# Where a prefix scan gets its first factor: from its own tile's front column, written one step ahead

## The chip, the cores and the metric

The kernel runs on one core of a Trainium2 chip. The metric is the device time of one execution in microseconds (us), the median of several runs. A profile is one further execution, recorded by the hardware profiler. Its engines are PE (TensorE matmuls), PEld (TensorE weight loads), DVE (VectorE), ACT (ScalarE), POOL (GpSimd) and SP (SyncE, which issues most DMAs).

## The reference, cut to what matters

One layer of an encoder over 2048 tokens of width 1024, in float32: a normed and modulated input, one input projection, two groups of eight attention heads of width 64, an output projection with a residual, and a squared-ReLU MLP. The change lies in the first group of heads, stick-breaking attention:

```
z = einsum(q, k) * scale                        # one row per query, one column per key
log_1m_beta = where(key < query, log_sigmoid(-z), 0)
suffix = cumsum(log_1m_beta, reverse) - log_1m_beta
w = where(key < query, exp(log_sigmoid(z) + suffix), 0)
out = w @ v
```

In products instead of logarithms: with f = sigmoid(-z), a running product p over the keys, from the nearest key to the farthest, gives the weight of a key as the product in front of it minus the product behind it. The kernel computes it so. The tokens stand in reverse order, so that "towards the past" is a scan from left to right.

## The kernel before, in words

The order of the work is written out by hand. First comes the input projection of the last block of tokens with the modulation (up to about 414 us from the start of the span), then the attention (to about 1300 us), in which matmuls of the remaining projections fill TensorE between the attention's own, then the MLP.

The attention is a list `units` (lines 1151 to 1154). A unit `SB(h, g, c)` is one stick-breaking head h, a block g of 512 queries and a block c of 512 keys; for one head and query block the units c = g, g+1, ... 3 follow one another. The unit with c = g is the diagonal one (`self.diag`), the others are called carried here, since their scan goes on from the last column of the unit before. A unit `CA(h, g)` is a head of the second group with softmax. Each unit has four steps, one for each 128 queries (`qi`). There are 80 stick-breaking units with 320 steps: 128 diagonal and 192 carried.

The loop over the steps (lines 1233 to 1267) emits for step i, in this order: the transposes of the weights of a unit eight steps back (`transposes`, TensorE, into PSUM tile `wt`); `soft1` of step i; for softmax units a scale on POOL; `parts`, which splits `wt` into `wth` (ACT) and `wtl` (DVE); the jobs left by the step before (`done`: copies of a finished accumulator on ACT and its sum `o` and split `os` on POOL, sums of squares `r` on POOL, evictions of the filling matmuls on ACT and DVE); the value matmuls `acc`; `scores` of step i+1 (TensorE, into PSUM tile `z`); and some filling matmuls. `z` and `wt` share four PSUM banks (line 95, and lines 759 and 817). Each engine works through its instructions in the order in which they are emitted.

`soft1` of a stick-breaking step (lines 822 to 840) is what the change touches. It takes a tile `pt` (named `p`, 513 columns, six buffers, line 680) and a tile `w` (named `b`). ACT replaces `z` by its sigmoid. POOL copies one column into `pt[:, 0:1]`: ones on the diagonal, or else `self.carry[qi]`, the last column of the product tile of four steps before. DVE scans: its first factor is the scalar operand, 1.0 on the diagonal, or else the carried column itself, read from the older tile; its products go to `pt[:, 1:n+1]`. POOL subtracts neighbouring columns of `pt` into `w`. On the diagonal step qi covers 512 - 128 qi columns, elsewhere 512.

The lines that the profile gives for these instructions are all that of a helper that records them (L42), so they are told apart by their tiles: `p<-z,p,zero` is a carried scan, `p<-z,masked` a diagonal one, `p<-p` and `p<-ones` are the copies, `b<-p` is the subtract.

Of the kernel before, what the change touches and what calls it, by code (L numbers as in the profile page):

```python
# [9 lines left out]
F32 = mybir.dt.float32  # L10
# [8 lines left out]
P = 128  # L19
# [6 lines left out]
TB = 512  # L26
# [53 lines left out]
def encoder_kernel(ctx, tc, xT, c, g1, g2, w_in, w_rest, gqk, bias, w_o, w1, w2, w_ada, b_ada, out):  # L80
    nc = tc.nc
    act, dve, pool, sp = nc.scalar, nc.vector, nc.gpsimd, nc.sync
# [34 lines left out]
    ones = cpool.tile([P, P], F32, name="ones")  # L117
# [121 lines left out]
    if True:  # L239
# [202 lines left out]
        def load_raws(*q):  # L442

            while loads and len(raws) - sum(len(wts.get(k, ())) >= (4 if k[1] < 4 else 4 * m + 4) for k, m in raws) < 3:
                load_raw(*loads.pop(0), *q)
# [42 lines left out]
        act, dve, pool = (Ordered(tc, e) for e in (act, dve, pool))  # L488
# [124 lines left out]
        def hook(job, n):  # L613

            if (job, n) == ((0, 3, 3), 1):
                dve.tensor_scalar_mul(gqk_s[:, 0:1], gqk_sb[:, 0:1], 0.125)
                dve.tensor_copy(gqk_s[:, 1:2], gqk_sb[:, 1:2])
                for p in range(2):
                    sp.dma_start(scr_w[p,], wide[:, :, :, p, :].bitcast(F32))
            if (job, n) == ((0, 6, 3), 2):  # L620
                norms.flush()
                end_norm(2, h_tile(2), 0, KT // 2)
            if (job, n) == ((0, 6, 3), 3):
                end_norm(2, hts[2], KT // 2, KT)
            if (job, n) == ((0, 6, 2), 1):
                load_x(1)
            if (job, n) == ((0, 4, 3), 0):
                start_norm(1, 5, 3)
            if (job, n) == ((0, 10, 2), 0):
                norms.flush()  # L630
                end_norm(1, h_tile(1))
                load_x(0)
                behind.add(2, lambda: start_norm(0, 3, 2))
            if (job, n) == ((1, 6, 1), 2):
                norms.flush()
                end_norm(0, h_tile(0), 0, KT // 2)
            if (job, n) == ((1, 6, 1), 3):
                end_norm(0, hts[0], KT // 2, KT)
            if (job, n) == ((1, 6, 0), 1):
                sp.dma_start(scr_h, whole[0].bitcast(F32))  # L640

        def run_job(n):
            nonlocal credit
            key, t = jobs[n][:2], jobs[n][2]
            last = n + 1 == len(jobs) or jobs[n + 1][:2] != key
            load_raws()
            if last and key != keys[-1]:
                after = keys[keys.index(key) + 1]
                coming.extend((after, m) for m in range(len(wts.get(after, ())), count[after]))
            bank = project(key, t, hts[t], last)  # L650
            for b in range(2 if key[1] < 4 else 4):
                hook(jobs[n], b)
                next(bank)
                behind.tick()
                norms.tick()
                later.tick()
                credit += (2.4 if key[0] else 1.65) if key[1] > 3 else 1.0 * key[0]
                while todo and credit > 0:
                    cost, job = todo.pop(0)
                    job()  # L660
                    credit -= cost
            for _ in bank:
                pass
            assert not coming
# [13 lines left out]
    if True:  # L678
        kp0 = ph.enter_context(tc.tile_pool(name="kp0", bufs=3, side="right"))
        zp = ph.enter_context(tc.tile_pool(name="zp", bufs=6, side="right"))  # L680
# [66 lines left out]
        class Unit:  # L747


            def __init__(self, h, g, first, last):  # L750
                self.h, self.g, self.first, self.last = h, g, first, last
                self.nm = f"{self.ca}_{h}_{g}"
                self.ws = []
                self.wt = {}

            def transposes(self, j):
                kb, q0, q1 = self.blocks[j]
                nm = f"{self.nm}_{kb}"
                wt = pz.tile([P, TB], F32, tag="z", name=f"wt{nm}")
                for qi in range(q0, q1):  # L760
                    pe.transpose(wt[:, qi * P : (qi + 1) * P], self.weights(qi, kb), ident)
                self.wt[j] = wt
# [22 lines left out]
        class SB(Unit):  # L785
# [10 lines left out]
            def load(self):  # L796
                if self.first:
                    pend["q"] = load_q(0, self.h, self.g)
                    pend["last"] = [None] * 4
                self.q = pend["q"]  # L800
                self.carry = pend["last"]
                self.k = self.shared("k", lambda: load_k(0, self.h, self.c, 1, f"{self.g}_{self.c}"))
# [4 lines left out]
            def shared(self, what, get):  # L807
# [2 lines left out]
                    pend[what] = get()  # L810
                return pend[what]

            def scores(self, qi):
                nm = f"{self.nm}_{qi}"
                c0 = qi * P if self.diag else 0
                n = TB - c0
                self.z = z = pz.tile([P, TB], F32, tag="z", name=f"z{nm}")
                qs = slice(qi * P, (qi + 1) * P)
                pe.matmul(z[:, :n], self.q[:, 0, qs], self.k[:, c0:], start=True, stop=False)
                pe.matmul(z[:, :n], self.q[:, 1, qs], self.k[:, c0:], start=False, stop=True)  # L820

            def soft1(self, qi):
                nm = f"{self.nm}_{qi}"
                c0 = qi * P if self.diag else 0
                n = TB - c0
                z = self.z
                w = zw.tile([P, TB], F32, tag="w", name=f"b{nm}")
                pt = zp.tile([P, TB + 1], F32, tag="p", name=f"p{nm}")
                act.activation(z[:, :n], z[:, :n], AF.Sigmoid, scale=-0.125)
                before = ones[:, 0:1] if self.diag else self.carry[qi]  # L830
                pool.tensor_copy(pt[:, 0:1], before)

                op, begin = (ALU.max, masked[:, :n]) if self.diag else (ALU.add, zero.to_broadcast([P, n]))
                dve.tensor_tensor_scan(
                    pt[:, 1 : n + 1], z[:, :n], begin, 1.0 if self.diag else before, op0=ALU.mult, op1=op,
                )

                pool.tensor_tensor(w[:, :n], pt[:, :n], pt[:, 1 : n + 1], op=ALU.subtract)
                self.carry[qi] = pt[:, n : n + 1]
                self.ws.append((w, c0))  # L840
# [310 lines left out]
        units = []  # L1151
# [50 lines left out]
        def value(u, j):  # L1202
            u.values(j)
# [5 lines left out]
        for _ in range(2):  # L1209
            filler[0].load()  # L1210
        run_job(len(jobs) - 1)
        units[0].scores(0)
        later.flush()
        pa.close()
# [15 lines left out]
        steps = [(u, st) for u in units for st in range(STEPS)]  # L1230

        turns = {STEPS * n: 4 if u.ca else 8 for n, u in enumerate(units) if n and u.ca != units[n - 1].ca}
        for i in range(len(steps) + LAG):
            if i % STEPS == 0:
                if i // STEPS + AHEAD < len(units):
                    load(units[i // STEPS + AHEAD])
            vi = i - VST
            if vi >= 0 and vi % STEPS == 0 and vi // STEPS < len(units):
                units[vi // STEPS].load_values()
            front, fs = steps[i] if i < len(steps) else (None, 0)  # L1240
            back, bs = steps[i - LAG] if i >= LAG else (None, 0)
            done = list(soon)
            soon.clear()
            js = []
            if back is not None:
                nb = len(back.blocks)
                js = range(nb * bs // STEPS, nb * (bs + 1) // STEPS)
            for j in js:
                back.transposes(j)
            if front is not None:  # L1250
                front.soft1(fs)
            while first:
                first.pop(0)()
            for j in js:
                back.parts(j)
                late.append((back, j))
            if front is not None:
                front.soft2(fs)
            for job in done:
                job()  # L1260
            while len(late) > AVLAG:
                value(*late.pop(0))
            if i + 1 < len(steps):
                u, st = steps[i + 1]
                u.scores(st)
            fill(front.weight if front else 0.6, turns.get(i, 0))
            later.tick()
# [26 lines left out]
    if True:  # L1294
# [35 lines left out]
        steps, jobs = [], {}  # L1330
# [514 lines left out]
        for mb in (1, 0):  # L1845
            begin = len(steps)
            steps += [First(mb, j, i) for j in range(NP) for i in OUTER]
            end = len(steps)
            for j in range(NP):
                f = steps[begin + 7 * j]  # L1850
# [33 lines left out]
        f = plain(0, 1)  # L1884
# [4 lines left out]
        for i, p in ((7, 6), (2, 5), (3, None), (4, None)):  # L1889
            f = outer(i, plan)  # L1890
# [109 lines left out]
```

## Time and profile before

| | |
|---|---|
| runs | 2566.47, 2568.27, 2568.61 us; median 2568.27 |
| the profiled execution | 2568.92 us |
| its span, first to last instruction | 2567.2 us |
| mean granted TensorE clock | 0.997 |
| scans on DVE | 192 carried, 245.7 us; 128 diagonal, 104.3 us |
| subtracts `b<-p` on POOL | 320, 292.5 us |
| copies into column 0 on POOL | 192 of a carried column, 36.0 us; 128 of ones, 23.7 us |

How to read the lines: in a list of groups, the mean duration in ns and the idle time of the engine ahead of the group follow the busy time, with what ended the idle time behind an arrow. In the order of time, a row has its start, its duration, the engine and the instruction with output and inputs; in brackets stands the idle time before it, and what ended it. Where an instruction waits for several others, the bracket names the one that came last by the profile, which can be a neighbour in time of the real one. `x2` at the end of a row means that two like instructions are merged into it.

### The profile page before, as it was taken

How to read it: one execution, taken by the hardware profiler on the slowest of the kernel's cores; microseconds unless marked ns; L12 is line 12 of the kernel's file. 1: busy time of each engine (PE TensorE's matmuls, PEld its weight loads, DVE VectorE, ACT ScalarE, POOL GpSimd, SP SyncE). 2: the span in 40 equal slices, each digit the busy share in tenths (PEclk: the TensorE clock that was granted, in tenths of full speed). 3: DMA queues.
4: the chain of work that ended last, by engine and by line, in shares of the span. 5: the costliest groups of instructions: out<-in, count | busy, mean ns of one | idle time of the engine just before them, and what ended most of it. 6: DMA issues, size and time to landing. Idle time of an engine off the chain costs nothing.

```text
span 2567.2 us, 39419 instructions
## 1 busy us (share of the span) xinstructions
PE 2534.1 (99%) x12436; PEld 2109.1 (82%) x12436; DVE 2012.0 (78%) x3501; ACT 1496.2 (58%) x2871; POOL 760.8 (30%) x1136
## 2 busy tenths in 40 slices
PE   9999999999999999999999999999999999999999
PEld 7888888888888888887887888888888878788887
DVE  7656767887789878998867777668978657988897
ACT  6333435668866687666755555566555545646565
POOL 4330145776776667777612000000000000000000
PEclk9999999999999999999999999999999999999999
DMA  9879978689877788756786888787899779677872
GB/s 351 332 298 363 342 281 293 213 237 290 277 239 233 238 279 272 248 193 196 224 309 243 286 285 274 260 306 267 275 323 304 273 254 409 246 272 265 291 268 82
DMA packets 293200, 698.92 MB, mean 272 GB/s; under 512 B 31360, under 2 KB 83584, under 8 KB 281856
## 3 DMA queue, kind: packets, MB, share of 16 engines
q1 hardware_dynamic: 291696, 691.69, 78.1%
q10 hardware_dynamic: 1296, 4.72, 0.5%
q8 instruction: 98, 1.61, 0.2%
q14 instruction: 110, 0.90, 0.1%
HBM read 477.66 MB, written 218.63 MB: 271 GB/s over the span
## 4 chain that ended last, share of the span: by engine, by line
PE 86%; DVE 5%; ACT 3%; DMA 2%; issue 2%; POOL 1%; SPq 1%; DVEq 0%; POOLq 0%; ACTq 0%
PE ps L42 29%; PE ps_s L42 14%; PE pt L42 11%; PE acc L42 6%; PE wt L42 6%; PE po L42 4%; PE z L42 4%; PE pf L42 4%; PE pq L42 3%; PE cz L42 2%; DVE p L42 2%; PE pso L42 1%; DVE opr L42 1%; PE ct L42 1%; ACT z L42 1%
## 5 line engine op out<-in xcount | busy, mean ns | idle before, releaser
L42 PE MATMUL ps<-h,opw 128*128 128x512 f32 x1512 | 361.7, 392 | 3.6 <-ACT cp L42 3.6
L42 ACT CAST wth<-wt 128x512 fp32r<-128x512 f32 (+3 forms) x544 | 257.4, 484 | 172.4 <-PE wt L42 162.5
L42 POOL TENSOR_TENSOR b<-p 128x512 f32<-128x512 f32 (+1 forms) x320 | 292.5, 914 | 167.9 <-DVE p L42 91.9
L42 PEld LDWEIGHTS ps<-h,opw 128*128 128x128 f32 x1512 | 285.7, 189 | 63.6 <-ACT cp L42 4.0
L42 DVE TENSOR_TENSOR wtl<-wt,wth 128x512 fp32r<-128x512 f32 (+3 forms) x544 | 291.2, 547 | 59.2 <-ACT wth L42 56.7
L42 PE MATMUL pt<-w,ht 128*128 128x512 f32 x1248 | 288.2, 391 | 0.0
L42 PE MATMUL ps_s<-h,opw 128*128 128x512 f32 x1152 | 278.6, 391 | 3.2 <-ACT ps_s L42 3.2
L42 PEld LDWEIGHTS pt<-w,ht 128*128 128x128 f32 x1248 | 233.0, 188 | 47.7
L42 PE MATMUL ps<-oph,opv 128*128 128x512 f32 x1152 | 263.8, 391 | 2.5 <-DVE txo L42 2.5
L42 DVE TENSOR_TENSOR_SCAN p<-z,p,zero 128x512 f32<-128x512 f32 x192 | 245.7, 1281 | 25.6 <-ACT z L42 18.6
L42 PEld LDWEIGHTS ps_s<-h,opw 128*128 128x128 f32 x1152 | 217.1, 189 | 48.8 <-ACT ps_s L42 3.6
L42 PEld LDWEIGHTS ps<-oph,opv 128*128 128x128 f32 x1152 | 217.2, 189 | 48.4 <-DVE txo L42 3.0
L42 PE MATMUL acc<-wth,v 128*128 128x512 f32 (+3 forms) x544 | 220.5, 409 | 0.0
L42 ACT CAST opr<-r 128x512 fp32r<-128x512 f32 x224 | 139.3, 623 | 107.7 <-PE ps L42 51.1
L42 ACT ACTIVATE z<-z 128x512 f32<-128x512 f32 (+1 forms) x320 | 166.5, 521 | 55.2 <-PE z L42 49.3
L42 PE MATMUL z<-k,q 128*128 128x512 f32 (+3 forms) x640 | 185.6, 372 | 7.7 <-DVE p L42 7.2
L42 PE MATMUL acc<-wtl,v 128*128 128x512 f32 (+3 forms) x544 | 185.4, 347 | 0.0
L42 PE MATMUL ps<-opr,ol 128*128 128x512 f32 x768 | 176.4, 389 | 0.1
L42 DVE TENSOR_TENSOR opr<-r,opr 128x512 fp32r<-128x512 f32 x224 | 151.2, 688 | 27.5 <-ACT opr L42 24.8
L42 PE MATMUL wt<-ident,b 128*128 128x128 f32 x1088 | 171.4, 273 | 1.1 <-DVE cols L42 0.3
L42 PEld LDWEIGHTS wt<-ident,b 128*128 128x128 f32 x1088 | 136.3, 140 | 42.2 <-DVE cols L42 1.8
L42 PEld LDWEIGHTS ps<-opr,ol 128*128 128x128 f32 x768 | 144.0, 188 | 30.5 <-DVE ol L42 0.4
(218 smaller groups left out, 4862.8 us busy)
## 6 DMA issues: line engine op xcount, KB each, us to landing
q<-scr_q SPq DMA_DIRECT2D x128, 256.0 KB, 4.7
w<-in_w_dram SPq DMA_DIRECT2D x64, 512.0 KB, 5.8
r<-scr_hid SPq DMA_DIRECT2D x64, 512.0 KB, 7.5
k<-scr_k SPq DMA_DIRECT2D x240, 128.0 KB, 4.3
v<-scr_v SPq DMA_DIRECT2D x120, 256.0 KB, 3.9
wa<-in_w_ada_dram SPq DMA_DIRECT2D x48, 512.0 KB, 6.4
ow<-scr_wo SPq DMA_DIRECT2D x24, 1024.0 KB, 5.8
hw<-scr_hid SPq DMA_DIRECT2D x48, 512.0 KB, 6.4
```

The costliest lines, as they stand in the source:

```text
L42: return lambda *x, **y: self.tc.keep_in_program_order(f(*x, **y))
```

## The change

A method `begin(qi)` takes the tile `pt` and emits the copy into its column 0. It is called for step i+1 in step i, behind the transposes and ahead of `soft1` of step i; for the very first step it is called ahead of the first scores. For softmax units it does nothing. `soft1` then picks the tile up, and a carried scan reads its first factor from `pt[:, 0:1]` and no longer from the older tile. The scalar of a diagonal scan stays the constant 1.0, as that line is not changed. The rest of `soft1` is not changed either.

```diff
+                self.pt = {}
+
+            def begin(self, qi):
+                pass
...
+            def begin(self, qi):
+                self.pt[qi] = pt = zp.tile([P, TB + 1], F32, tag="p", name=f"p{self.nm}_{qi}")
+                pool.tensor_copy(pt[:, 0:1], ones[:, 0:1] if self.diag else self.carry[qi])
+
...
-                pt = zp.tile([P, TB + 1], F32, tag="p", name=f"p{nm}")
+                pt = self.pt.pop(qi)
                 act.activation(z[:, :n], z[:, :n], AF.Sigmoid, scale=-0.125)
-                before = ones[:, 0:1] if self.diag else self.carry[qi]
-                pool.tensor_copy(pt[:, 0:1], before)
+                before = pt[:, 0:1]
...
+        units[0].begin(0)
         units[0].scores(0)
...
             for j in js:
                 back.transposes(j)
+            if i + 1 < len(steps):
+                steps[i + 1][0].begin(steps[i + 1][1])
             if front is not None:
                 front.soft1(fs)
```

## The prediction, made before the changed kernel had run

> **What bounds the kernel now.** I read the head of the profile first, then the busy time by stage, then who waits for whom, and last the order of time at the scans. All times are us from the start of the span.
>
> ```profile
> PE 2534.1 (99%) x12436; PEld 2109.1 (82%) x12436; DVE 2012.0 (78%) x3501; ACT 1496.2 (58%) x2871; POOL 760.8 (30%) x1136
> ```
>
> TensorE is busy for 99% of the span, so a change in another engine counts only where TensorE's queue, which runs strictly in program order, stands still for it. The next row is the first stage with scans, by window (its length, then busy time of PE, PEld, DVE, ACT, POOL, then the granted clock).
>
> ```profile
> 414.00:500.00 86.00, 83.73 (x469) 70.07 (x468) 74.57 (x107) 56.99 (x122) 61.15 (x117) 1.00 0.83 251
> ```
>
> DVE is busy for 74.57 of 86 us, 87%: it is the engine with the least room behind TensorE. The longest of the waits of TensorE's weight loads while scans and softmax run, and the work on the scan's tile `p`, show how the two are tied:
>
> ```profile
> PEld z L42 <- DVE p L42: 14.1, 27, 1.3
> ```
>
> ```profile
> L42 POOL TENSOR_TENSOR b<-p x320: 400/1042/1046, 416.2 to 1207.2; 128x512 f32<-128x512 f32 x128, 128x256 f32<-128x256 f32 x32
> L42 DVE TENSOR_TENSOR_SCAN p<-z,p,zero x192: 1260/1284/1289, 417.9 to 1205.8; 128x512 f32<-128x512 f32 x192
> ...
>   POOL p L42: 5.5, 9
> ```
>
> 27 times the weights of a score matmul `z` wait for a scan, 14.1 us in all, 1.3 at the longest. Four PSUM banks are shared by `z` and `wt`, one of each per step, so the scores for step k+2 take the bank that scan k frees. A late scan stops TensorE once it is later than the room before that load. The last row is idle time of DVE ahead of a scan that a copy on POOL is said to have ended: 5.5 us in 9 places, so today the scans hardly wait for POOL.
>
> **The change part by part.** *Number of instructions.* Nothing is added: one copy per scan stays, at 0.18 to 0.19 us (the COPY rows below); 320 scans and 320 subtracts stay. No DMA is issued by what is moved, and POOL issues none in this stage; SP's queue is untouched. If POOL's work were on the path, moving them would change nothing in its sum.
>
> *The copy's new place.* POOL's queue is now copy k, subtract k, whatever `done` brings (sums `o`, `os`, `r`), copy k+1, subtract k+1. After the change copy k+1 stands ahead of subtract k, behind the jobs of step k-1; that is the slot where copy k stands now. It is moved past one subtract and, where there are any, one step's `done` jobs or softmax scale. Could it hold up the subtract behind it? It needs scan k-3 and the old readers of its buffer, all older than scan k, for which that subtract waits anyway. I take 0; without this cover it would cost 0.19 us on POOL, once per step, beside a subtract.
>
> *The new wait.* A carried scan (192 of 320) reads its first factor from column 0 of its own tile, which POOL writes. Before, it took the factor from the older tile, written by DVE. Now scan k needs copy k. The diagonal scans (128) keep the constant 1.0 in the call and gain no wait. That a carried scan does not need its copy now is seen where it starts first:
>
> ```profile
> 417.91 4.81 DVE L42 TENSOR_TENSOR_SCAN p<-z,p,zero 128x512 f32<-128x512 f32 x4
> ...
> 419.09 0.19 POOL L42 COPY p<-ones 128x1 f32<-128x1 f32 x1
> ...
> 419.70 0.19 POOL L42 COPY p<-p 128x1 f32<-128x1 f32 x1
> ...
> 422.63 1.20 DVE L42 TENSOR_TENSOR_SCAN p<-z,masked 128x512 f32<-128x512 f32 x1
> ...
> 423.89 0.30 PEld L42 LDWEIGHTS z<-k,q 128*128 128x128 f32 x2 [0.30 <-DVE p L42]
> ```
>
> The scan at 417.91 runs 1.8 us ahead of its copy at 419.70. DVE may run ahead of POOL by what the six `p` buffers allow; the change cuts this to about one step. Queued behind a waiting scan on DVE are the step's `wtl` subtraction, the evictions of the dense banks (`stf`, `svf`, `xr`) and the next scan; TensorE waits for all of them.
>
> *What an ordinary step pays: nothing.*
>
> ```profile
> 714.46 0.19 POOL L42 COPY p<-p 128x1 f32<-128x1 f32 x1
> ...
> 715.48 1.28 DVE L42 TENSOR_TENSOR_SCAN p<-z,p,zero 128x512 f32<-128x512 f32 x1
> ```
>
> The scan at 715.48 would need the copy that stands where the one of 714.46 does; it ends at 714.65, 0.83 early. The cover is that step's DVE and ACT work. I made this comparison for all 192 carried scans (start against the end of the copy one place ahead, plus 0.05 for the handoff): 28 come too early, by 15.7 us in sum. The first is the one at 417.91, the last this:
>
> ```profile
> 1191.98 1.28 DVE L42 TENSOR_TENSOR_SCAN p<-z,p,zero 128x512 f32<-128x512 f32 x1
> ...
> 1192.09 0.19 POOL L42 COPY p<-p 128x1 f32<-128x1 f32 x1
> ```
>
> *Term 1, the first unit: 1.7 us.* The scan of 417.91 gets its copy at 419.09+0.19+0.05 = 419.33, so 1.4 late. The four scans ran at a pitch of 1.20 (4.81/4); now a subtract of 1.04, a copy of 0.19 and the handoffs stand between every second one of them and the next, which I put at 0.3 more in all, so the scan of 422.63 is 1.7 late. The weights at 423.89 already wait for its end: no cover.
>
> *Term 2, the worst place: 1.6 us.*
>
> ```profile
> 1173.71 1.27 DVE L42 TENSOR_TENSOR_SCAN p<-z,p,zero 128x512 f32<-128x512 f32 x1
> ...
> 1175.04 0.42 PEld L42 LDWEIGHTS z<-k,q 128*128 128x128 f32 x2
> ...
> 1175.32 0.18 POOL L42 COPY p<-p 128x1 f32<-128x1 f32 x1
> ```
>
> Here POOL comes late because two sums of other jobs (`r` and `o`) stand between the subtract and this copy. The copy's place ends at 1175.50, so the scan would start at 1175.55, 1.84 late. The weights of 1175.04 follow the scan's present end (1174.98) by 0.06, so there is no room and all of it reaches the weight loads. A matmul still in flight hides about one load (half of the 0.42 that the two take): 1.6 is left.
>
> *Terms 3 and 4, two smaller places: 0.6 + 0.4 us.*
>
> ```profile
> 723.81 1.28 DVE L42 TENSOR_TENSOR_SCAN p<-z,p,zero 128x512 f32<-128x512 f32 x1
> ...
> 724.31 0.18 POOL L42 COPY p<-p 128x1 f32<-128x1 f32 x1
> ...
> 725.14 0.38 PEld L42 LDWEIGHTS z<-k,q 128*128 128x128 f32 x2
> ```
>
> ```profile
> 823.61 1.28 DVE L42 TENSOR_TENSOR_SCAN p<-z,p,zero 128x512 f32<-128x512 f32 x1
> ...
> 824.81 0.18 POOL L42 COPY p<-ones 128x1 f32<-128x1 f32 x1
> ...
> 825.92 0.42 PEld L42 LDWEIGHTS z<-k,q 128*128 128x128 f32 x2
> ```
>
> At 723.81 the copy's place gives 724.31+0.18+0.05 = 724.54, so the scan is 0.73 late; from its present end (725.09) to the load there is 0.05 of room, and matmuls in flight hide a little more: 0.6. At 823.61 the scan is 825.04-823.61 = 1.43 late, and the room from 824.89 to 825.92 is 1.03: 0.4. This is the place of the sum `os`, on POOL once per two heads.
>
> *Term 5, the other early scans: 1.7 us.* None of them by itself is late by more than 0.4 beyond its room. But DVE has little idle time, so lateness is handed on to the scans behind it, and the room there can be smaller. Bounds: 0, and what is left of the 15.7 when the lateness of the six scans of terms 1 to 4 is taken off (the four in a row at 417.91 are 1.4 late at the first and 4.2 in all): 15.7-4.2-1.84-0.73-1.43 = 7.5. I take 1.7, the nearer to 0, as the ordinary step has room to spare, and the row of 14.1 us says that TensorE is already stopped by about one scan in twelve.
>
> *Sum:* 1.7+1.6+0.6+0.4+1.7 = 6 us more. Behind the last scan TensorE is as full as before (99% over the span), so nothing is given back. Against the profiled execution (2568.92, a span of 2567.2 and 1.7 around it) that is 2574.9; against the median of the three runs, 2568.27, it is **2574.3**.
>
> **The rivals.** *Hidden.* TensorE's load of `z` has more room than I think, or DVE catches up at once; only terms 1 and 2 stay, partly: 0 to 3 us, 2568.3 to 2571.3. For it: 164 of 192 carried scans have slack. Against it: the 27 waits above.
>
> *All of the lateness arrives.* 9 to 15.7 us, 2577 to 2584. For it: DVE at 87%. Against it: the rooms of 1.03 in term 4 and 0.83 in the ordinary step.
>
> *Faster: POOL's copies free the buffers sooner.* A scan also waits until the last reader of its buffer, a copy two steps back, is done; that copy now comes a step earlier, so the 5.5 us of waits on copies above may go, and at most that arrives: 2562.8 to 2568. It decides if POOL really ended those waits. The longest of them on a carried scan speaks against it:
>
> ```profile
> 1169.48 0.58 ACT L42 ACTIVATE z<-z 128x512 f32<-128x512 f32 x1
> ...
> 1170.15 1.28 DVE L42 TENSOR_TENSOR_SCAN p<-z,p,zero 128x512 f32<-128x512 f32 x1 [1.25 <-POOL p L42]
> ```
>
> The sigmoid of the same scan ends at 1170.06, 0.09 ahead of it, so without POOL the scan would start no sooner, and 1.25 of the 5.5 are not POOL's.
>
> *The clock gate.* A longer hole in TensorE's work could lower its clock. The granted clock is 1.00 in the window above, which has 2.3 us of holes; the longest single wait is 1.3, and with all of term 2's 1.84 on top it would be 3.1. If the clock halved for as long as such a hole, 3 us of matmuls would take 3 us more: 2577. The Trainium skill, "TensorE: Matmul & The Clock Gate", section "What's actually happening", says that the array falls to half its clock after an idle window of about 3.4 us. By that rule, no hole here gets there; no run here shows the threshold itself.
>
> *The change does nothing:* were the wait on the copy already there by way of the buffer, the time would stay. The 1.8 us lead at 417.91 excludes it for that scan.
>
> **How the numbers follow.** A measurement of this kernel tells about 0.2%, 5.1 us, from no change. Forecast (3 to 9 us more) 0.59, of which 0.41 above 5.1; hidden or nothing 0.24; all arrives 0.09; clock gate 0.01; faster 0.07, of which 0.03 by over 5.1. That gives slower 0.41+0.09+0.01 = 0.51, faster 0.03, same 0.46. The range leaves out the faster case and the upper half of the case where all arrives: 2568.5 to 2579.
>
> **What would show it.** Right: in the changed profile each carried scan starts after its own copy; near 418 the first of them waits about 1.4 us on POOL and the scans behind it come apart; waits of carried scans on POOL `p` rise from 5.5 to some 15; the weights of `z` wait for scans some 6 us longer in all than 14.1; the copies stand ahead of the previous step's subtract; after 1300 nothing differs but the shift. Wrong: waits of `z` at 14 or less, or a shift that arises in another stage. A scan of another length than 1.284 would break the sum too.

## The result, and the profile after

The changed kernel takes 2572.38 us (median of ten runs, 2569.52 to 2577.33) against 2568.50 for the kernel before (ten runs beside it, 2565.39 to 2571.80): a ratio of 1.0017, 95% interval 1.0009 to 1.0025. A second set of runs gave 1.0014 (1.0005 to 1.0023), though its median is only 1.8 us higher; the ratios here are not the quotients of the medians. Both intervals lie above 1: the change costs some 2 to 4 us, at most a quarter of a per cent. The profiled execution has a span of 2570.8, against 2567.2 before.

The head of the changed kernel's profile, and the first stage with scans (length, busy time of PE, PEld, DVE, ACT, POOL with the number of instructions, granted clock, and last the DMA share and rate):

```profile
PE 2534.4 (99%) x12436; PEld 2106.9 (82%) x12436; DVE 2010.5 (78%) x3501; ACT 1496.5 (58%) x2871; POOL 755.3 (29%) x1136
```

```profile
414.00:500.00 86.00, 82.83 (x463) 69.07 (x462) 73.80 (x106) 55.96 (x120) 59.63 (x114) 1.00 0.84 250
```

TensorE's busy time is the same as before to 0.3 us (2534.1); the span has grown by idle time. The weights of the score tile `z` wait longer for scans, 19.1 us in 36 places instead of 14.1 in 27:

```profile
PEld z L42 <- DVE p L42: 19.1, 36, 1.9
```

The work on tile `p` after the change, with the idle time of DVE behind POOL's copies in its last line (before: 5.5 us, 9 places):

```profile
L42 POOL TENSOR_TENSOR b<-p x320: 391/1042/1049, 415.3 to 1209.9; 128x512 f32<-128x512 f32 x128, 128x256 f32<-128x256 f32 x32
...
L42 DVE TENSOR_TENSOR_SCAN p<-z,p,zero x192: 1258/1283/1289, 418.2 to 1208.5; 128x512 f32<-128x512 f32 x192
...
  POOL p L42: 14.5, 24
```

A scan is as long as before (1283 ns against 1284); it comes later. A yardstick for single executions is the stretch from the first to the last weight load of `z`. Here are the kernel before, the changed one, and the changed one's second profile (the run `again` below), in three fences:

```profile
L42 PEld LDWEIGHTS z<-k,q x640: 186/188/193, 412.6 to 1203.0; 128*128 128x128 f32 x160
```

```profile
L42 PEld LDWEIGHTS z<-k,q x640: 186/188/193, 411.8 to 1205.7; 128*128 128x128 f32 x160
```

```profile
L42 PEld LDWEIGHTS z<-k,q x640: 186/188/193, 412.0 to 1205.7; 128*128 128x128 f32 x160
```

That is 790.4, 793.9 and 793.7 us: 3.3 to 3.5 us more, against 3.6 to 4.4 by the ratios of the times and 1.8 to 3.9 by their medians. What lies ahead of and behind the stretch is 0.1 us longer than before in the first profile and 1.6 shorter in the second, so no cost of the same sign in both is left outside it.

The start of the scans in the changed kernel, in order of time:

```profile
417.37 0.61 POOL L42 TENSOR_TENSOR b<-p 128x256 f32<-128x256 f32 x1
417.93 0.19 POOL L42 COPY p<-p 128x1 f32<-128x1 f32 x1
418.07 0.40 POOL L42 TENSOR_TENSOR b<-p 128x128 f32<-128x128 f32 x1
418.15 5.03 DVE L42 TENSOR_TENSOR_SCAN p<-z,p,zero 128x512 f32<-128x512 f32 x4 [1.16 <-POOL p L42]
...
422.06 0.30 PEld L42 LDWEIGHTS z<-k,q 128*128 128x128 f32 x2 [0.68 <-DVE p L42]
...
424.34 0.30 PEld L42 LDWEIGHTS z<-k,q 128*128 128x128 f32 x2 [0.80 <-DVE p L42]
```

The copy of the first carried scan now stands ahead of the subtract of the step before it (418.07), the scan waits 1.16 us for it and starts 0.03 behind its end (418.12), and two loads of `z` wait where one did.

The worst place, around 1177:

```profile
1175.59 1.28 POOL L42 TENSOR_TENSOR o<-o,otmp 64x512 f32<-64x512 f32 x1
...
1176.93 0.18 POOL L42 COPY p<-p 128x1 f32<-128x1 f32 x1
...
1177.15 1.28 DVE L42 TENSOR_TENSOR_SCAN p<-z,p,zero 128x512 f32<-128x512 f32 x1 [1.73 <-POOL p L42]
...
1178.49 0.30 PEld L42 LDWEIGHTS z<-k,q 128*128 128x128 f32 x2 [1.88 <-DVE p L42]
1178.49 0.73 PE L42 MATMUL z<-k,q 128*128 128x512 f32 x2 [1.45 <-DVE p L42]
```

Read upwards it is the mechanism: the matmul waits for the scan, the scan for the copy, the copy for the sum `o` that has nothing to do with it.

### The profile page after: what moved, and what is told of

Read it like the earlier page. It is cut to its first block, busy times and chain, and to the rows that moved or that the text cites. A ratio compares the mean times of both kernels' runs of the same rounds, so it can differ in the third digit from the quotient of the medians.

```text
span 2570.8 us, 39492 instructions
## 1 busy us (share of the span) xinstructions
PE 2534.4 (99%) x12436; PEld 2106.9 (82%) x12436; DVE 2010.5 (78%) x3501; ACT 1496.5 (58%) x2871; POOL 755.3 (29%) x1136
## 4 chain that ended last, share of the span: by engine, by line
PE 84%; DVE 6%; DMA 3%; ACT 3%; issue 2%; SPq 1%; POOL 1%; DVEq 0%; ACTq 0%; POOLq 0%
PE ps L42 27%; PE ps_s L42 13%; PE pt L42 11%; PE acc L42 6%; PE wt L42 6%; PE po L42 4%; PE z L42 4%; PE pf L42 4%; PE pq L42 3%; PE cz L42 2%; DVE p L42 2%; PE pso L42 1%; DVE wtl L42 1%; PE ct L42 1%; DVE opr L42 1%
```

## The experiments

The theory was that the time is lost where a carried scan waits for its own copy, because the copy stands in POOL's queue behind work of an earlier step. The rivals were that the copy's new place is what costs, that reading the factor from the scan's own tile costs something by itself, and that the tiles run out when they are taken earlier. Times are medians, against runs of the kernel before on the same chip: 2568.85 for `again`, `copy_ahead_old_factor`, `two_steps_ahead` and `ahead_of_the_jobs`, 2568.78 for `same_step` and `copy_on_act`, 2569.28 for `two_steps_more_rounds`, `first_unit_old_factor` and `jobs_and_first_unit`.

**`again`**, the changed kernel itself:

> The changed kernel once more, timed beside the next three on one chip, as the yardstick for them. If the first result holds: 3 to 6 us over the kernel before, ratio 1.001 to 1.0025, with 15 to 24 carried scans that start right behind their own copy.

2570.64 us, ratio 1.0014 (1.0005 to 1.0023); 24 carried scans start within 0.12 us behind their copy (22 in the first profile). The ratio and the count are as expected; the median is 1.8 us over the kernel before, less than the 3 to 6 expected.

**`copy_ahead_old_factor`**: the copy is moved, the dependence is not made.

```diff
-                    pt[:, 1 : n + 1], z[:, :n], begin, 1.0 if self.diag else before, op0=ALU.mult, op1=op,
+                    pt[:, 1 : n + 1], z[:, :n], begin, 1.0 if self.diag else self.carry[qi], op0=ALU.mult, op1=op,
```

> The copy is one step ahead as in the change, but the carried scan takes its factor from the older tile as before. Theory (the cost is the scan's wait for its own copy on POOL): as the kernel before, ratio 0.9990 to 1.0008, waits of z's weights for scans back to about 14 us, scans again starting ahead of their own subtract's neighbours, the first carried scan near 417. Rival (the cost is the copy's new place in POOL's queue, or the shifted program): as the changed kernel, ratio 1.0012 to 1.0025, waits of z's weights near 19 us.

2568.88 us, ratio 1.0001 (0.9992 to 1.0009). Its waits and its start, from two views:

```profile
PEld z L42 <- DVE p L42: 13.6, 27, 1.3
```

```profile
417.09 4.81 DVE L42 TENSOR_TENSOR_SCAN p<-z,p,zero 128x512 f32<-128x512 f32 x4
...
417.95 0.18 POOL L42 COPY p<-p 128x1 f32<-128x1 f32 x1
```

The copies stand where the change puts them, the scans overtake them again, and the cost is gone. So it is the wait and not the place. As to the faster rival, DVE's idle time behind POOL copies falls from 5.5 to 2.8 us, and the median does not follow; an interval of some 2 us either way leaves room for a small gain.

**`same_step`**: the opposite half, the dependence with the copy left in its own step.

```diff
-                pt = self.pt.pop(qi)
+                pt = zp.tile([P, TB + 1], F32, tag="p", name=f"p{nm}")
                 act.activation(z[:, :n], z[:, :n], AF.Sigmoid, scale=-0.125)
+                pool.tensor_copy(pt[:, 0:1], ones[:, 0:1] if self.diag else self.carry[qi])
                 before = pt[:, 0:1]
```

> The copy stays in its own step, as in the kernel before, and only the factor comes from the scan's own column. Theory: copy k stands behind subtract k-1, which waits for scan k-1, so each of the 192 carried scans stands in one serial loop of scan 1.28, subtract 1.04, copy 0.19 and three handoffs of 0.05 to 0.1, about 2.7 us, against some 1.8 us per step now; 192 times 0.9 is 170 us, less at the 48 first steps of a unit behind short subtracts, more where a sum stands between: 100 to 200 us over the kernel before, and nearly every carried scan begins behind its own copy. Rival (the source of the factor costs little, the place of the copy is what counts): within 6 us of the kernel before.

2723.87 us, a single run, 155 more. The waits on tile `p`, and a few steps in order of time:

```profile
  POOL p L42: 180.8, 175
```

```profile
1189.02 1.28 DVE L42 TENSOR_TENSOR_SCAN p<-z,p,zero 128x512 f32<-128x512 f32 x1 [0.90 <-POOL p L42]
...
1190.45 1.04 POOL L42 TENSOR_TENSOR b<-p 128x512 f32<-128x512 f32 x1 [1.46 <-DVE p L42]
1191.44 0.18 POOL L42 COPY p<-p 128x1 f32<-128x1 f32 x1
1191.65 1.28 DVE L42 TENSOR_TENSOR_SCAN p<-z,p,zero 128x512 f32<-128x512 f32 x1 [0.44 <-POOL p L42]
...
1193.08 1.04 POOL L42 TENSOR_TENSOR b<-p 128x512 f32<-128x512 f32 x1 [1.46 <-DVE p L42]
1194.07 0.18 POOL L42 COPY p<-p 128x1 f32<-128x1 f32 x1
1194.29 1.28 DVE L42 TENSOR_TENSOR_SCAN p<-z,p,zero 128x512 f32<-128x512 f32 x1 [1.17 <-POOL p L42]
```

Scan, subtract, copy, scan: one serial loop of 2.64 us a step (1194.29-1191.65), in which DVE and POOL take turns; 179 of 192 carried scans start right behind their copy. The step ahead in the change is what keeps this loop open, almost.

**`two_steps_ahead`** and **`two_steps_more_rounds`**: the same kernel in two sets of runs.

```diff
+        units[0].begin(1)
...
-            if i + 1 < len(steps):
-                steps[i + 1][0].begin(steps[i + 1][1])
+            if i + 2 < len(steps):
+                steps[i + 2][0].begin(steps[i + 2][1])
```

> The scan takes its factor from its own column, and the copy is made two steps ahead instead of one. Theory: the copy then stands one step's jobs earlier in POOL's queue and nearly every scan finds it done; at most the first unit pays up to 1 us; ratio 0.9990 to 1.0010, idle time of scans behind POOL copies below 6 us. Rival (the product tiles, six of them, run out when they are taken earlier): ratio above 1.0015, and scans or copies that wait for the release of a tile.

> Two steps ahead once more, as its interval (0.9999 to 1.0016) holds both answers while its profile shows no cost in the attention stage. Theory: ratio 0.9990 to 1.0008 and again at most 0.5 us in the stretch of the scores. Rival (taking the tiles earlier costs): ratio above 1.001.

2570.50 us, ratio 1.0008 (0.9999 to 1.0016), then 2569.31, ratio 1.0000 (0.9991 to 1.0009). The first profile has

```profile
L42 PEld LDWEIGHTS z<-k,q x640: 186/188/193, 413.1 to 1203.0; 128*128 128x128 f32 x160
```

a stretch of 789.9 us, 0.5 shorter than before, and 4.3 us of idle time behind copies. The first set of runs alone held both answers; with the second there is no cost left to see, though one of some 2 us is not excluded. The second profile's stretch is longer, 791.6 us (412.4 to 1204.0), so 1.2 over before and not the 0.5 at most that was expected. The reason has nothing to do with scans: a window of it runs at a granted clock of 0.97.

```profile
600.00:650.00 50.00, 48.53 (x290) 41.70 (x289) 36.36 (x137) 40.85 (x104) 36.67 (x35) 0.97 0.86 265
```

The first has 1.00 there. Inside the window the clock is at half for 3.4 us. The difference of the two stretches is 1.7 us, taken here as an estimate of what such a fall costs; it agrees with 3.4 us at half speed, and between the weight loads on either side of the fall the second profile loses 1.6 us against the kernel before. The last section comes back to it.

**`ahead_of_the_jobs`**: the copy of step i+2 right behind the subtract of step i. That is ahead of the sums, but not ahead of one more subtract.

```diff
+        units[0].begin(1)
...
-            if i + 1 < len(steps):
-                steps[i + 1][0].begin(steps[i + 1][1])
             if front is not None:
                 front.soft1(fs)
+            if i + 2 < len(steps):
+                steps[i + 2][0].begin(steps[i + 2][1])
```

> The copy for step i+2 stands right behind the subtract of step i and ahead of the sums o, os and r of that step, so between the place of the change and that of two steps ahead. Theory, with the prediction's terms: the places where a sum keeps POOL (near 723, 823, 868, 1173) cost nothing now, the first unit near 418 still costs its 1.3 to 1.7 us, as no sum stands there: ratio 1.0002 to 1.0012. Rival (the one-step loop from subtract to copy to scan is what costs, not the sums): as the changed kernel, ratio 1.0012 to 1.0025.

2571.23 us, ratio 1.0009 (0.9998 to 1.0019), which does not decide. The profile does. Near 1177 the copy now runs ahead of the sums, and the scan starts in time:

```profile
1174.07 0.18 POOL L42 COPY p<-p 128x1 f32<-128x1 f32 x1
1174.20 1.28 POOL L42 TENSOR_TENSOR r<-r,sq 128x512 f32<-128x512 f32 x1
...
1175.21 1.28 DVE L42 TENSOR_TENSOR_SCAN p<-z,p,zero 128x512 f32<-128x512 f32 x1
```

Only 5 carried scans start right behind their copy. The stretch of the scores (411.4 to 1204.7) is 793.3 us with a fall to half clock in it; less 1.7 it is 791.6, 1.2 over before, a little under the 1.3 to 1.7 that the theory has for the first unit alone.

**`first_unit_old_factor`**: the change, but the first carried unit reads its factor as before.

```diff
-1.0 if self.diag else before
+1.0 if self.diag else self.carry[qi] if self is units[1] else before
```

> The change, but the four scans of the first carried unit (near 418) take their factor from the older tile as before; 188 scans keep the new wait. Theory (the cost is a sum over single places, and the first unit is one of the two large ones): the stretch from the first to the last score, 3.3 to 3.5 us longer than before in the two profiles of the change, is 1.3 us shorter than there, so 2.0 to 2.3 longer than before, if no half-clock stretch falls into it; ratio 1.0002 to 1.0015. Rival (TensorE makes up for a late start later in the attention stage): the stretch stays 3.3 to 3.5 longer.

2571.04 us, ratio 1.0010 (1.0001 to 1.0019), which does not decide. Its stretch is 793.9 us (412.0 to 1205.9), no shorter than in the change, but its clock from 600 to 650 is 0.97, so an estimated 792.2 without that: 1.8 over before, a little under the 2.0 to 2.3 expected, and 1.5 to 1.7 under the change. One comparison needs no such correction. Ahead of the fall, the load of `cz` (the score tile of the softmax units) that starts at 612.13 in the change starts at 611.10 here; counted from the first load of `z` (411.78 and 412.05) that is 1.3 us earlier, as much as the first unit costs. So none of it is made up for in the 190 us behind the first unit.

**`jobs_and_first_unit`**: both edits.

> Both large causes out: the copy stands ahead of the sums, two steps ahead, and the four scans near 418 take their factor from the older tile; 188 scans read their own column. Theory: nothing of the cost is left, the stretch from the first to the last score within 0.8 us of before (a half-clock stretch in it would add 1.5 to 1.7), ratio 0.9990 to 1.0008. Rival (a read of the own column costs something by itself): ratio above 1.001 as in the change.

2569.67 us, ratio 1.0002 (0.9993 to 1.0011), with

```profile
L42 PEld LDWEIGHTS z<-k,q x640: 186/188/193, 412.1 to 1202.4; 128*128 128x128 f32 x160
```

790.3 us, 0.1 under before, at full clock. 188 scans read their own column here, at no cost that shows, so the read by itself is not what costs.

**`copy_on_act`**: another engine for the copy.

```diff
-                pool.tensor_copy(pt[:, 0:1], ones[:, 0:1] if self.diag else self.carry[qi])
+                act.copy(pt[:, 0:1], ones[:, 0:1] if self.diag else self.carry[qi])
```

> As the change, but ACT makes the 320 copies in place of POOL. On ACT the copy of step k stands ahead of the sigmoid of step k-1, and a scan waits for its own sigmoid anyway. Theory: the wait for the copy is then always over when the scan's sigmoid is; what is left is ACT's own time, 320 times some 0.2 to 0.3 us in stages where ACT is busy for two thirds, so sigmoids come a little later: 0 to 8 us over the kernel before. Rival (any factor that another engine writes makes the scan late by a handoff): at least the 4 us of the change, with scans starting 0.05 us behind a copy.

2573.70 us, ratio 1.0018 (1.0006 to 1.0030). Two of its rows on tile `p`:

```profile
L42 ACT COPY p<-p x192: 173/194/214, 415.8 to 1205.3; 128x1 f32<-128x1 f32 x192
...
  ACT p L42: 3.4, 3
```

As expected no carried scan starts within 0.12 us behind its copy. The last row is idle time that a copy on ACT ended, 3.4 us in three places, none of them ahead of a carried scan. ACT now has 320 copies of 0.19 us more, 62 us in all, and the scores' stretch (412.1 to 1206.9) is 4.4 us longer. That the cost comes through later sigmoids is argued and not shown.

None of these kernels is faster than the one before; the best are level with it.

## Why the prediction was right, and which terms were too large

The forecast was 6 us more, 2574.3; it came out at some 4, 2572.4, inside the range and nearer to the kernel before. The range says little by itself, as its lower end of 2568.5 is the median of the kernel before; and the even chance that the forecast gave to more than 5.1 us was too high. What bears it out is the mechanism: the copy moved, all 192 carried scans start behind their own copy, some began to wait for it, and TensorE's loads waited for the scans. `copy_ahead_old_factor` shows no cost of the new place alone, `jobs_and_first_unit` none of the read alone. The forecast of DVE's idle time behind copies (some 15 us) met 14.5; that of the loads' waits (6 longer) met 5.0. The shift arises in the attention stage. The terms can be read from the loads of `z`, whose place in the two profiles is compared from their first load on, 412.62 and 411.78, so that an equal place is a difference of -0.84.

*Term 1, 1.7 us; measured 1.3* (424.34 against 423.89). The first scan is 1.1 us late and not 1.4. The handoffs were well put: the four scans take 5.03 instead of 4.81 us, 0.22 for my 0.3. The copy came sooner than its place said. A subtract used to begin only when the copy just ahead of it in POOL's queue had ended, and it reads that copy; now the copy ahead of it is another tile's. The rows before are

```profile
418.27 0.19 POOL L42 COPY p<-ones 128x1 f32<-128x1 f32 x1
...
418.54 0.62 POOL L42 TENSOR_TENSOR b<-p 128x256 f32<-128x256 f32 x1
```

From the start of the copy to that of the subtract it was 0.27 there, and is 0.14 now (417.93 to 418.07). In the whole profile of the kernel before it is never under 0.25. POOL gains 0.13 a step at places where it is the one that is late. I had moved the copy and left the spacing as it was.

*Term 2, 1.6 us; measured 1.0 to 1.1.* Ahead of the place the load at 1173.30 before starts at 1174.94 after, 1.64 later; behind it the load at 1177.84 starts at 1180.43, 2.59 later, and from the next load but one on it is 2.7. The matmul of the scores stands idle for 1.45 us at 1178.49. But in the kernel before there was idle time one pair of loads later, and that is gone:

```profile
1177.84 0.62 PE L42 MATMUL z<-k,q 128*128 128x384 f32 x2 [0.35 <-DVE p L42]
```

A hole put ahead of an older one swallows part of it. The term took off a load in flight, and not the hole behind.

*Term 3, 0.6; measured 0.1.* Just ahead of the place the two profiles stand level. The load came late as forecast, by 0.7, and four steps later most of it is made up for: the rows of the two kernels, before and after, are

```profile
723.50 0.30 PEld L42 LDWEIGHTS z<-k,q 128*128 128x128 f32 x2
...
731.53 0.42 PEld L42 LDWEIGHTS z<-k,q 128*128 128x128 f32 x2
```

```profile
723.51 0.30 PEld L42 LDWEIGHTS z<-k,q 128*128 128x128 f32 x2
...
725.85 0.30 PEld L42 LDWEIGHTS z<-k,q 128*128 128x128 f32 x2 [0.78 <-DVE p L42]
...
731.65 0.42 PEld L42 LDWEIGHTS z<-k,q 128*128 128x128 f32 x2
```

From 0.0 at the first row to 0.7 at the copy (725.85 against the 725.14 of the forecast's row) to 0.1. *Term 4, 0.4; measured below 0.1.* The scan waits as said, 1.07 us:

```profile
824.94 1.28 DVE L42 TENSOR_TENSOR_SCAN p<-z,p,zero 128x512 f32<-128x512 f32 x1 [1.07 <-POOL p L42]
...
826.28 0.30 PEld L42 LDWEIGHTS z<-k,q 128*128 128x128 f32 x2 [0.24 <-DVE p L42]
```

Its load waits 0.24 us, and no idle time of the matmuls follows: they had that much in hand. *Term 5, 1.7 by judgement:* 3.3 to 3.5 less the others, 2.4 to 2.6, leaves 0.7 to 1.1. Load by load, some 0.6 and 0.2 of it arise near 1055 and 1117, where a scan waits 0.48 us for a copy behind a sum `o`; so one place cost more than the 0.4 that was allowed to any. Another 0.6 (0.3 in the second profile) arises near 975, where no scan waits for its copy; its cause stays open. Against this, 0.4 is gained between 424 and 586. (The 28 early scans, added up again, come to 15.4 us and not 15.7, which lowers the upper bound of this term to 7.2.)

So terms 2 to 4 were too large by the same oversight: lateness beyond the room ahead of a load was taken to reach TensorE almost in full, and what TensorE has in flight and what holes stand behind was hardly taken off. Term 1 missed the copy's shorter spacing instead. Of the rivals, "hidden" was the nearest in size, just under what was measured with its 0 to 3 us. "All of the lateness arrives" fell: 9.0 us more of idle time behind copies became 3.3 to 3.5 of time. "Faster" does not hold for the change, but a small gain from the copy's place is not excluded: the stretch of `copy_ahead_old_factor` (411.8 to 1202.5) is 790.7 us with a fall to half clock in it, so an estimated 789.0 without, 1.4 under before, in one profile. "Does nothing" fell with the first wait of 1.16 us.

The clock-gate rival did not come about in the changed kernel's attention stage. Its granted clock is 1.00 in the windows from 414 to 1213.6, also in the one that holds the hole of 1.45 us:

```profile
1100.00:1213.60 113.60, 110.40 (x602) 90.22 (x601) 103.15 (x134) 73.51 (x137) 79.55 (x127) 1.00 0.62 201
```

But the reason that the forecast gave from the Trainium skill's rule does not hold, as the last section shows, and a fall costs some 1.7 us and not the 3 that this rival was priced at.

## What to carry to other kernels

Before a value's source is moved from one engine to another, look at who stands in the new engine's queue ahead of it: an instruction of 0.19 us makes its reader wait for all the unrelated work there. Compare each reader's start in the trace with the end of the place that the writer will have; here 28 of 192 came too early, and a few of these carry most of the cost. Then take off, for each, the work that the bounding engine has in flight and any hole that already stands close behind.

## What the runs showed of the hardware

TensorE's clock can fall to half for 3.4 us after a hole much shorter than that. In `ahead_of_the_jobs`, four windows of 3.4 us in a row, of which the second holds one wait of 1.05 us (the row below them) and is busy for 2.26 us:

```profile
613.80:617.20 3.40, 3.31 (x26) 2.93 (x25) 2.00 (x6) 3.40 (x10) 3.33 (x4) 1.00 1.04 293
617.20:620.60 3.40, 2.26 (x17) 1.90 (x17) 3.14 (x13) 2.44 (x10) 2.28 (x4) 1.00 0.90 302
620.60:624.00 3.40, 3.40 (x15) 3.10 (x15) 2.04 (x8) 2.19 (x6) 1.59 (x3) 0.50 0.95 325
624.00:627.40 3.40, 3.40 (x20) 2.91 (x20) 1.79 (x7) 1.74 (x6) 1.85 (x2) 1.00 1.05 264
```

```profile
618.52 0.44 PE L42 MATMUL cz<-k,q 128*128 128x128 f32 x2 [1.05 <-DVE cols L42]
```

The profile of the kernel before has the same hole of 1.05 us, at 618.56, and no fall behind it. So the same hole is followed by a fall in one execution and not in another. The traces say a little about where. In each profile the falls start at whole multiples of 3.413 us from one another. With windows of that length counted from the falls, the hole lies wholly inside one window in the four profiles that have a fall near 619 (617.47 to 618.52 in 617.17 to 620.58 here), and each time the fall follows at that window's end; in the kernel before, a boundary at 618.03 cuts the hole in two halves of 0.5 us. But in the changed kernel the hole, 617.55 to 618.59, lies inside one window too (615.51 to 618.92), and no fall follows. So its place in the window does not decide alone, and the rest stays open. The Trainium skill, "TensorE: Matmul & The Clock Gate", section "What's actually happening", gives an idle window of about 3.4 us as the condition. The length of 3.4 us and the half clock agree with the trace; an idle window of that length was not needed. At some 1.7 us each, these falls are about half as large as the change that was measured here: when single profiles are compared in steps of a microsecond, the granted clock of each window has to be read first.
